# Layer 0 of a two-layer decoder trunk: twenty conv taps and seven weight low parts move to GpSimd, and the diagonal tap products leave TensorE

## The chip, the cores and the metric

The kernel runs on one core of one Trainium2 chip. A core has five engines that run side by side, each in its own order: TensorE (PE, matrix products, with weight loads PEld beside them), VectorE (DVE), ScalarE (ACT), GpSimd (POOL) and SyncE (SP, which here issues the DMAs). The metric is the device time of one execution in microseconds (us), lower being better. Times of runs are medians; the profile is of one execution.

## What is computed

Two layers over 512 tokens of 1024 channels, all in float32. The part that matters here is the mixer of layer 0:

```python
proj = h @ w_in
a, g = proj[..., :CONV_CH], proj[..., CONV_CH:c0]
u = a * jax.nn.sigmoid(g)
u = causal_dwconv(u, conv_w, conv_b)
u = jax.nn.silu(layernorm(u, conv_ln_g, conv_ln_b))
...
q = (rmsnorm(cq, q_norm_g) @ w_uq).reshape(B, S, MLA_HEADS, QK_NOPE + QK_ROPE)
...
o = mla_attention(qn, qr, kn, kr, v)
return jnp.concatenate([u, o], axis=-1) @ w_out
```

The causal depthwise convolution has 31 taps on 512 channels: each output channel is a sum of 31 shifted copies of its own input channel, each times one number. Beside it stand eight heads of causal attention, and both go through one output projection. After the mixer comes a gated MLP with a 3-tap conv; layer 1 is a pooling mixer and another MLP.

## The kernel before

Channels lie on the 128 partitions, the 512 tokens along the free dimension. Every large product is made of three: each float32 operand is split into a high part (rounded, made by ScalarE) and a low part (the rest, made by VectorE), and `mm3` (L107) issues high by high, high by low and low by high into one PSUM bank. `split` (L96) makes such a pair.

**Weights** come in chunks of up to 128x1024 in the order of `stream` (L130). `fetch` issues a chunk's DMA on SyncE, `prepare` splits it, `weights()` hands it out and keeps one chunk prepared ahead. The raw chunk, its high and its low part have three buffers each. Chunk 18 is the first of w_uq, 19 and 20 are w_ukv, 21 to 23 the other three of w_uq (called uq1, uq2, uq3 below; 768 columns; each serves the queries of two heads), 24 to 31 w_out (1024 columns).

**The convolution** has four tiles of 128 channels. `glu` (L429) makes the input u of a tile (its last step, L439, is on VectorE) and calls `conv` (L375), which puts closures on lists; `pump` takes some from the lists and so decides where in the program a tap stands. Tiles 0, 1 and 2 begin with tap 30 and the bias on ScalarE (L383, into a PSUM bank with the tag conv) and add taps 0 to 29 on VectorE (L400, one instruction a tap). `close` copies the sum to `side`. Tile 3 does taps 0 to 15 on TensorE: GpSimd makes a diagonal matrix with the tap's 128 weights (L392), and TensorE multiplies u by it in full float32 into the bank aux (L393); VectorE adds taps 16 to 30, and `close` adds the bias. Tiles 0 and 1 get their u early, tile 2 at about 85 us, tile 3 at about 97 us.

**The attention** goes head by head: `scores(h)`, for even heads the keys of the next pair (`keys_of`), `transposes(h-1)`, `queries(h+2)`, `values(h-2)`. Inside `scores`, `pump(BLK, i % 2)` takes two entries of the VectorE list after each of four blocks, and one entry of the TensorE list after every second. `queries(h)` multiplies the w_uq chunk with three tiles of the query latent.

**After the heads** the four conv tiles are transposed on TensorE (L623), normalized over the channels on VectorE (L625 to L637), transposed back (L648) and multiplied with the second half of w_out.

A scheduler puts each engine's instructions into one fixed order when the program is built; at run time an engine waits at an instruction until its inputs are there, and everything behind it on that engine waits too.

Of the kernel before, what the change touches and what calls it, by code (L numbers as in the profile page):

```python
# [8 lines left out]
F32 = mybir.dt.float32  # L9
F32R = mybir.dt.float32r  # L10
I32 = mybir.dt.int32
AF = mybir.ActivationFunctionType
ALU = mybir.AluOpType
AX = mybir.AxisListType

P = 128
S = 512
# [5 lines left out]
CW = 31  # L23
# [9 lines left out]
C_NE, C_CB, C_LG, C_LB, C_QG, C_KG, C_NO, C_PS, C_NF, C_FN = 0, 8, 12, 16, 20, 23, 25, 33, 41, 57  # L33
# [3 lines left out]
N_COL = C_FB + 2 * NF  # L37

WARM = 40
PE_TAPS = 16  # L40
W_PAD, T_PAD, R_PAD = 48, 16, 120
GLU, LAT, BLK, END = 3, 4, 2, 0

# [2 lines left out]
def kernel(  # L46
# [20 lines left out]
    act, dve, pool, pe = nc.scalar, nc.vector, nc.gpsimd, nc.tensor  # L67
# [11 lines left out]
    def uid(s):  # L79
        count[0] += 1  # L80
        return f"{s}{count[0]}"

    def bank():
        return p_ps.tile([P, S], F32, tag="ps", name=uid("ps"))

    def aux(tag="aux"):
        return p_ps.tile([P, S], F32, tag=tag, bufs=1, name=uid(tag))

    def temp():
        return p_t.tile([P, 2 + S], F32, tag="t", name=uid("t"))[:, :S]  # L90

    def small(n=4, dt=F32):
        return p_s.tile([P, 8], dt, tag=f"s{dt}", name=uid("s"))[:, :n]


    def split(dst, src):  # L96
        i = act.copy(dst[0], src)  # L97
        dve.tensor_tensor(dst[1], src, dst[0].bitcast(F32), op=ALU.subtract)  # L98
        return i

    def split_scaled(dst, src, scale):
# [40 lines left out]
    raws, ready = [], []  # L142
# [3 lines left out]
    def fetch():  # L146
        src, n = stream[len(raws)]
        raw = p_w.tile([P, 1024], F32, tag="raw", name=uid("raw"))[:, :n]
        nc.sync.dma_start(raw, src)
        raws.append(raw)  # L150

    def prepare():
        i = len(ready)
        if i == len(raws):
            fetch()
        n = stream[i][1]
        hi = p_w.tile([P, 1024], F32R, tag="hi", name=uid("hi"))[:, :n]
        lo = p_w.tile([P, 1024], F32R, tag="lo", name=uid("lo"))[:, :n]
        copied = split((hi, lo), raws[i])
        raws[i] = None  # L160
        ready.append((hi, lo))
        return copied

    def weights(ahead=1):
        given[0] += 1
        while len(ready) < min(given[0] + ahead, len(stream)):
            prepare()
        w = ready[given[0] - 1]
        ready[given[0] - 1] = None
        return w  # L170
# [18 lines left out]
    def c(i):  # L189
        return col[:, i : i + 1]  # L190

    sq = p_c.tile([P, 3, P], F32, name="sq")
    ident, ones, fold_kr = sq[:, 0, :], sq[:, 1, :], sq[:, 2, :]
# [80 lines left out]
    p_m = tc.alloc_tile_pool(name="mixer", bufs=1, side="left", reuse_waits="tile")  # L274
# [8 lines left out]
    for k in range(KD):  # L283
        xk = p_x.tile([P, S], F32, tag="x", name=uid("x"))
        nc.sync.dma_start(xk, xT[k * P : (k + 1) * P, :])
        x.append(xk)
        fetch()
        if k < 3:
            opened = prepare()
        split_scaled(pair(xg[k]), xk, c(C_NE + k))  # L290
# [63 lines left out]
    for k in range(KD):  # L354
        w = weights(2)
# [8 lines left out]
    def project():  # L364
        w = weights()
        ps = bank()
        for k in range(KD):
            mm3(ps, part(w, k), pair(xg[k]), k == 0, k == KD - 1)
        return ps

    u, ys, work, pe_work = [], [], [], []

    def conv(m):  # L375
        cw = C_CW + CW * m
        side = p_m.tile([P, S], F32, tag="side", bufs=4, name=uid("side"))
        ys.append(side)
        st = {}

        def open_acc():
            st["acc"] = aux("conv")
            act.activation(  # L383
                st["acc"], u[m][:, CW - 1 : CW - 1 + S], AF.Identity,
                bias=c(C_CB + m), scale=c(cw + CW - 1),
            )

        def pe_tap(j):
            if j == 0:
                st["acc"] = aux()  # L390
            d = p_m.tile([P, P], F32, tag="tapped", bufs=4, name=uid("tap"))
            pool.tensor_scalar(d, ident, c(cw + j), None, op0=ALU.mult)  # L392
            pe.matmul(st["acc"], d, u[m][:, j : j + S], start=j == 0, stop=j == PE_TAPS - 1)  # L393

        def tap(j):
            while m == 3 and pe_work:
                pe_work.pop(0)()
            if not st:
                open_acc()
            i = dve.scalar_tensor_tensor(  # L400
                st["acc"], u[m][:, j : j + S], c(cw + j), st["acc"],
                op0=ALU.mult, op1=ALU.add,
            )
            if held:
                tc.add_manual_dep(
                    i.ins, held.pop().ins.name,
                    mybir.DependencyInfo(
                        mybir.DependencyClass.NoSync, mybir.DependencyReason.DATA
                    ),
                    reason="background",  # L410
                )

        def close():
            bias = c(C_CB + m) if m == 3 else 0.0
            act.activation(side, st["acc"], AF.Identity, bias=bias, scale=1.0)

        n_pe = PE_TAPS if m == 3 else 0
        pe_work.extend((lambda j=j: pe_tap(j)) for j in range(n_pe))
        work.extend((lambda j=j: tap(j)) for j in range(n_pe, CW if m == 3 else CW - 1))
        work.append(close)  # L420

    def pump(nd, np_=0):
        for _ in range(min(np_, len(pe_work))):
            pe_work.pop(0)()
        for _ in range(min(nd, len(work))):
            work.pop(0)()


    def glu(ps_a, ps_g):  # L429
        t = temp()  # L430
        dve.tensor_tensor(t, ps_g, rows0, op=ALU.mult)
        s = temp()
        act.activation(s, t, AF.Sigmoid)
        if len(u) == 3:
            act.activation(spare, s[:, 0:1], AF.Exp)
        dve.tensor_tensor(s, s, rows0, op=ALU.mult)
        ut = p_m.tile([P, 640], F32, tag="u", bufs=4, name=uid("u"))[:, : CW - 1 + S]
        pool.memset(ut[:, : CW - 1], 0.0)
        dve.tensor_tensor(ut[:, CW - 1 :], ps_a, s, op=ALU.mult)  # L439
        u.append(ut)  # L440
        conv(len(u) - 1)
# [6 lines left out]
    def latent(n, gain, width):  # L448
        parts, stat = [], Squares(width, dve)
        for m in range(n):  # L450
            ps = project()
            parts.append(s4())
            split_scaled(pair(parts[m]), ps, c(gain + m))
            stat.add(ps)
            pump(LAT)
        return parts, stat
# [11 lines left out]
    for _ in range(2):  # L468
        ps_a = project()
        pump(GLU)  # L470
        ps_g = project()
        glu(ps_a, ps_g)
        pump(GLU)
    p_xg.release()
    p_a = tc.alloc_tile_pool(name="attn", bufs=1, side="right", reuse_waits="tile")
    keys = [p_m.tile([P, 2, S], F32, tag="k", bufs=2, name=f"keys{i}") for i in range(2)]
# [26 lines left out]
    def scores(h):  # L503
        q, key = qs.pop(h), keys[h // 2 % 2][:, h % 2, :]
        pb = p_a.tile([P, 1280], F32, tag="prob", bufs=3, name=uid("prob"))
        mx, nb, ls = small(), small(), small()
        blocks, at = [], 0
        for i in range(4):
            w = (i + 1) * P
            ps = bank()  # L510
            pe.matmul(ps[:, :w], q[:, i * P : (i + 1) * P], key[:, :w], start=True, stop=True)  # L511
            p = pb[:, at : at + w]
            at += w
            dve.tensor_tensor_reduce(
                out=p, in0=ps[:, :w], in1=causal[:, S - w :], scale=1.0,
                scalar=-3.0e38, op0=ALU.add, op1=ALU.max, accum_out=mx[:, i : i + 1],
            )
            blocks.append(p)
            if i % 2:
                two = slice(i - 1, i + 1)  # L520
                dve.scalar_tensor_tensor(
                    nb[:, two], mx[:, two], -1.0, q_scale[:, two], op0=ALU.mult, op1=ALU.mult
                )
                for n in (i - 1, i):
                    act.activation(
                        blocks[n], blocks[n], AF.Exp, bias=nb[:, n : n + 1],
                        scale=q_scale[:, n : n + 1], accum_out=ls[:, n : n + 1],
                    )
            pump(BLK, i % 2)
        dve.reciprocal(ls, ls)  # L530
        for i in range(4):
            act.activation(blocks[i], blocks[i], AF.Copy, scale=ls[:, i : i + 1])
        probs[h] = blocks
        sums[h] = ls[:, 3:4]
# [85 lines left out]
    for i in range(4):  # L620
# [3 lines left out]
        st = p_s.tile([P, 6], F32, tag="bn", bufs=2, name=uid("bn"))  # L624
# [11 lines left out]
    for i in range(4):  # L636
        dve.tensor_scalar(  # L637
            yts[i], yts[i], mv[:, i, 0:1], r_ln[:, i : i + 1],
            op0=ALU.subtract, op1=ALU.mult,
# [3 lines left out]
    for m in range(4):  # L643
# [5 lines left out]
        t = temp()  # L649
# [183 lines left out]
    for h in range(2):  # L833
        w = weights()
        for i in range(4):
# [11 lines left out]
            if (h, i) >= (0, 2):  # L847
                while zps:
                    i, ps = zps.pop(0)
# [151 lines left out]
```

## Time and profile before

| | |
|---|---|
| median of 3 runs | 991.12 us (990.99 to 994.11) |
| the profiled execution's own time | 992.3 us |
| its span, first to last instruction | 990.5 us |
| mean granted TensorE clock | 0.993 |
| DVE instructions, busy | 915, 591.3 us |
| POOL instructions, busy | 107, 70.7 us |

The times of single instructions below are from the profiled execution, whose own time is 1.2 us above the median. A row of a timeline gives the start in the span, the duration (of all instructions merged in the row), the engine, the line, the operation, what it writes and reads, and in brackets the idle time before it and who ended it. Durations of instructions that follow each other can overlap; the distance between two starts is then what one costs. A row of the chain gives the start, the time that the chain spent there, and the line. A row of windows gives busy time of PE, PEld, DVE, ACT and POOL in a stretch of time, each with the number of instructions, then the granted clock, the DMA share and GB/s.

### The profile page before, as it was taken

Reading aid. Unit: us, or ns where it says so; the run is one execution under the profiler, and the core shown is the slowest. Engines: PE = TensorE matmul, PEld = TensorE weight load, DVE = VectorE, ACT = ScalarE, POOL = GpSimd, SP = SyncE. Lnnn points to the kernel's source line nnn. Section 1 sums busy time; section 2 is a strip of 40 time slices with the busy share of each in tenths; the row PEclk is TensorE's granted clock in tenths of the full one; section 3 lists DMA queues with packets and bytes.
Section 4 is the critical chain, followed back from the end, with each engine's and each line's share of the span. In section 5 each row is a group of like instructions: output and inputs, shape, how many; then the busy total and the mean of one; then the engine's idle time right before and its main releaser. Section 6 shows DMA issues by size and latency. Waiting matters only on the chain.

```text
span 990.5 us, 11545 instructions
## 1 busy us (share of the span) xinstructions
PE 973.5 (98%) x4476; PEld 799.1 (81%) x4476; DVE 591.3 (60%) x915; ACT 400.6 (40%) x581; POOL 70.7 (7%) x107
## 2 busy tenths in 40 slices
PE   8999999999999999999999999999999999999996
PEld 7788676777888888888888889888888888888885
DVE  6899989847675656555332338585656565522323
ACT  6534677544343333334222236253333333332321
POOL 6000100003000000000001102200000000000111
PEclk9999999999999999999999999999999999999998
DMA  6422101113233232322323241323232323323212
GB/s 216 157 81 90 48 18 65 36 49 109 84 107 107 85 107 93 98 94 98 100 92 107 86 158 44 107 86 106 85 107 86 106 87 105 100 92 106 86 43 85
DMA packets 29478, 91.99 MB, mean 93 GB/s; under 512 B 4080, under 2 KB 6384, under 8 KB 29424
## 3 DMA queue, kind: packets, MB, share of 16 engines
q1 hardware_dynamic: 28880, 90.74, 28.1%
q8 instruction: 35, 0.57, 0.3%
q10 hardware_dynamic: 544, 0.52, 0.2%
q14 instruction: 19, 0.16, 0.0%
HBM read 89.02 MB, written 2.23 MB: 92 GB/s over the span
## 4 chain that ended last, share of the span: by engine, by line
PE 93%; DVE 4%; DMA 1%; issue 1%; SPq 0%; ACT 0%; DVEq 0%
PE ps L108 28%; PE ps L109 28%; PE ps L110 28%; PE ps L558 2%; PE ps L511 2%; DVE lo L98 1%; PE aux L393 1%; PE ps L546 1%; PE aux L261 1%; PE aux L239 1%; DMA x<-in_xT_dram 0%; DVE xgl L103 0%; DMA col<-in_cols_dram 0%; PE ps L870 0%; PE ps L869 0%
## 5 line engine op out<-in xcount | busy, mean ns | idle before, releaser
L108 PE MATMUL ps<-xgh,hi 128*128 128x512 f32 x816 | 319.3, 391 | 2.0 <-ACT hi L97 1.8
L97 ACT CAST hi<-raw 128x1024 fp32r<-128x1024 f32 (+2 forms) x166 | 170.0, 1026 | 373.7 <-PE ps L109 351.5
L110 PE MATMUL ps<-xgh,lo 128*128 128x512 f32 x816 | 318.0, 390 | 0.8 <-DVE lo L98 0.8
L109 PE MATMUL ps<-xgl,hi 128*128 128x512 f32 x816 | 318.4, 390 | 0.0
L98 DVE TENSOR_TENSOR lo<-raw,hi 128x1024 fp32r<-128x1024 f32 (+2 forms) x166 | 201.6, 1216 | 153.8 <-ACT hi L97 153.3
L108 PEld LDWEIGHTS ps<-xgh,hi 128*128 128x128 f32 x816 | 153.8, 188 | 34.5 <-ACT hi L97 2.6
L110 PEld LDWEIGHTS ps<-xgh,lo 128*128 128x128 f32 x816 | 153.5, 188 | 33.4 <-DVE lo L98 2.0
L109 PEld LDWEIGHTS ps<-xgl,hi 128*128 128x128 f32 x816 | 153.7, 188 | 31.8
L108 PE MATMUL ps<-gh,hi 128*128 128x512 f32 (+1 forms) x374 | 141.1, 377 | 0.0
L109 PE MATMUL ps<-gl,hi 128*128 128x512 f32 (+1 forms) x374 | 140.9, 377 | 0.0
L110 PE MATMUL ps<-gh,lo 128*128 128x512 f32 (+1 forms) x374 | 140.8, 376 | 0.0
L108 PEld LDWEIGHTS ps<-gh,hi 128*128 128x128 f32 x374 | 70.4, 188 | 13.0
L110 PEld LDWEIGHTS ps<-gh,lo 128*128 128x128 f32 x374 | 70.4, 188 | 13.0
L109 PEld LDWEIGHTS ps<-gl,hi 128*128 128x128 f32 x374 | 70.4, 188 | 12.7
L698 DVE TENSOR_TENSOR t<-ps,rows 128x512 f32<-128x512 f32 x44 | 30.4, 691 | 76.9 <-PE ps L110 76.9
L226 POOL TENSOR_TENSOR sqr<-sqr,sqr 128x512 f32<-128x512 f32 x33 | 50.4, 1529 | 314.4 <-ACT sqr L224 284.5
L710 DVE TENSOR_TENSOR t<-ps,rows 128x512 f32<-128x512 f32 x44 | 30.4, 690 | 67.3 <-PE ps L110 67.0
L400 DVE SCALAR_TENSOR_TENSOR conv<-u,col,conv 128x512 f32<-128x512 f32 x90 | 67.5, 750 | 1.7 <-ACT conv L383 0.7
L705 DVE SCALAR_TENSOR_TENSOR t<-t,col,t 128x512 f32<-128x512 f32 x88 | 65.7, 748 | 1.4
L708 ACT ACTIVATE t<-t 128x512 f32<-128x512 f32 x44 | 27.8, 631 | 74.4 <-DVE t L705 74.4
L103 DVE SCALAR_TENSOR_TENSOR xgl<-x,col,xgh 128x512 fp32r<-128x512 f32 x32 | 32.7, 1037 | 12.4 <-ACT xgh L102 12.3
L108 PE MATMUL ps<-s,hi 128*128 128x512 f32 x96 | 39.7, 427 | 0.0
(182 smaller groups left out, 817.1 us busy)
## 6 DMA issues: line engine op xcount, KB each, us to landing
raw<-in_w_up_dram SPq DMA_DIRECT2D x88, 512.0 KB, 3.3
raw<-in_w_down_dram SPq DMA_DIRECT2D x44, 512.0 KB, 3.3
raw<-in_w_in_dram SPq DMA_DIRECT2D x10, 512.0 KB, 3.4
raw<-in_w_out_dram SPq DMA_DIRECT2D x8, 512.0 KB, 3.3
x<-in_xT_dram SPq DMA_DIRECT2D x8, 256.0 KB, 4.4
raw<-in_w_in_dram SPq DMA_DIRECT2D x8, 256.0 KB, 3.4
raw<-in_w_uq_dram SPq DMA_DIRECT2D x4, 384.0 KB, 3.0
raw<-in_w_ukv_dram SPq DMA_DIRECT2D x2, 512.0 KB, 3.8
```

The source lines that it names most:

```text
L97: i = act.copy(dst[0], src)
L98: dve.tensor_tensor(dst[1], src, dst[0].bitcast(F32), op=ALU.subtract)
L103: dve.scalar_tensor_tensor(dst[1], src, scale, dst[0].bitcast(F32), op0=ALU.mult, op1=ALU.subtract)
L108: pe.matmul(ps, a[0], b[0], start=start, stop=False)
L109: pe.matmul(ps, a[0], b[1], start=False, stop=False)
L110: pe.matmul(ps, a[1], b[0], start=False, stop=stop)
L226: self.engine.tensor_tensor(self.parts[0], self.parts[0], t, op=ALU.add)
L400: i = dve.scalar_tensor_tensor(st["acc"], u[m][:, j : j + S], c(cw + j), st["acc"], op0=ALU.mult, op1=ALU.add,)
L698: dve.tensor_tensor(ut[:, 2 : 2 + S], pu, rows, op=ALU.mult)
L705: dve.scalar_tensor_tensor(a, ut[:, j : j + S], c(fw + j * NF + f), a, op0=ALU.mult, op1=ALU.add)
L708: act.activation(a, a, AF.Silu)
L710: dve.tensor_tensor(b, pv, rows, op=ALU.mult)
```

## The change

`PE_TAPS` goes, and with it the diagonal matrices and their products. Tile 3 is now opened on ScalarE like the other tiles. Of tiles 2 and 3, taps 0 to 9 are made by GpSimd: the first multiplies u by the tap's column, spread along the tokens, straight into `side`; the others multiply into one of two buffers and then add to `side`. VectorE makes taps 10 to 29, and `close` adds its PSUM sum to `side` there. The low parts of chunks 21 to 27 (uq1 to uq3 and four chunks of w_out) are made by GpSimd. GpSimd taps are pumped two after each gate of the second pair of tiles, then one after each score block.

```diff
-PE_TAPS = 16
+POOL_TAPS = (0, 0, 10, 10)
+POOL_LOW = range(21, 28)
...
-    def split(dst, src):
+    def split(dst, src, engine=None):
         i = act.copy(dst[0], src)
-        dve.tensor_tensor(dst[1], src, dst[0].bitcast(F32), op=ALU.subtract)
+        (engine or dve).tensor_tensor(dst[1], src, dst[0].bitcast(F32), op=ALU.subtract)
...
-        copied = split((hi, lo), raws[i])
+        copied = split((hi, lo), raws[i], pool if i in POOL_LOW else dve)
...
-        def pe_tap(j):
-            if j == 0:
-                st["acc"] = aux()
-            d = p_m.tile([P, P], F32, tag="tapped", bufs=4, name=uid("tap"))
-            pool.tensor_scalar(d, ident, c(cw + j), None, op0=ALU.mult)
-            pe.matmul(st["acc"], d, u[m][:, j : j + S], start=j == 0, stop=j == PE_TAPS - 1)
+        def pool_tap(j):
+            t = side
+            if j:
+                t = p_m.tile([P, S], F32, tag="tapped", bufs=2, name=uid("tapped"))
+            w = c(cw + j).to_broadcast([P, S])
+            pool.tensor_tensor(t, u[m][:, j : j + S], w, op=ALU.mult)
+            if j:
+                pool.tensor_tensor(side, side, t, op=ALU.add)
...
         def close():
-            bias = c(C_CB + m) if m == 3 else 0.0
-            act.activation(side, st["acc"], AF.Identity, bias=bias, scale=1.0)
-
-        n_pe = PE_TAPS if m == 3 else 0
-        pe_work.extend((lambda j=j: pe_tap(j)) for j in range(n_pe))
-        work.extend((lambda j=j: tap(j)) for j in range(n_pe, CW if m == 3 else CW - 1))
+            if n_pool:
+                dve.tensor_tensor(side, st["acc"], side, op=ALU.add)
+            else:
+                act.copy(side, st["acc"])
+
+        n_pool = POOL_TAPS[m]
+        pool_work.extend((lambda j=j: pool_tap(j)) for j in range(n_pool))
+        work.extend((lambda j=j: tap(j)) for j in range(n_pool, CW - 1))
...
-        pump(GLU)
+        pump(GLU, 2)
...
-            pump(BLK, i % 2)
+            pump(BLK, 1)
```

Lines after the first edit are one, later three, higher than before: L98 becomes L99, L400 becomes L401, L511 becomes L514.

In the order of GpSimd, the changed program has these rows from the last taps of tile 2 to the first of tile 3. `u_807` is tile 2's input and `u_889` tile 3's; `side_810` and `side_892` are their sums; `lo_979` is the low part of uq1.

```order
L394 TENSOR_TENSOR tapped_1099<-u_807,col 128x512
L396 TENSOR_TENSOR side_810<-side_810,tapped_1055 128x512
L396 TENSOR_TENSOR side_810<-side_810,tapped_1099 128x512
L394 TENSOR_TENSOR tapped_1110<-u_807,col 128x512
L396 TENSOR_TENSOR side_810<-side_810,tapped_1110 128x512
L99 TENSOR_TENSOR lo_979<-raw_976,hi_978 128x768
L394 TENSOR_TENSOR side_892<-u_889,col 128x512
L394 TENSOR_TENSOR tapped_1127<-u_889,col 128x512
```

Nineteen rows of tile 2 (ten multiplies, nine adds) stand ahead of `lo_979`; before, the low part of uq1 was VectorE's, right behind the last gate's u. The same engine ends tile 3 so, with uq2's low part (`lo_1077`), uq3's (`lo_1242`) and the first of w_out (`lo_1414`) behind all nineteen rows of tile 3:

```order
L394 TENSOR_TENSOR tapped_1302<-u_889,col 128x512
L396 TENSOR_TENSOR side_892<-side_892,tapped_1302 128x512
L99 TENSOR_TENSOR lo_1077<-raw_1074,hi_1076 128x768
L99 TENSOR_TENSOR lo_1242<-raw_1239,hi_1241 128x768
L99 TENSOR_TENSOR lo_1414<-raw_1411,hi_1413 128x1024
```

Before, the low part of uq2 (then `lo_1062`) stood on VectorE among the score blocks of head 0 (`prob_1008`):

```order
L514 ISA prob_1008,s_1009<-ps_1017,causal 128x256
L514 ISA s_1009 128x1
L98 TENSOR_TENSOR lo_1062<-raw_1059,hi_1061 128x768
L521 SCALAR_TENSOR_TENSOR s_1010<-s_1009,misc 128x2
L514 ISA prob_1008,s_1009<-ps_1029,causal 128x384
```

It has moved from the blocks of head 0 on one engine to the end of tile 3's taps on another.

On TensorE, the program before has this around scores(2), the keys (`ps_1188`), the transposes of head 1 and queries(4), which read uq2:

```order
L393 MATMUL aux_1023<-u_885,tap_1162 128x512
L511 MATMUL ps_1167<-keys_899,q_1075 128x384
L511 MATMUL ps_1172<-keys_899,q_1075 128x512
L393 MATMUL aux_1023<-u_885,tap_1178 128x512
L108 MATMUL ps_1188<-s_626,hi_903 128x512
```

and the changed one this from the last key product (`ps_1213`) over the transposes (L549) to the first product with `lo_1077`:

```order
L111 MATMUL ps_1213<-s_666,lo_914 128x512
L549 MATMUL ps_1223<-sq,prob_1092 128x128 x4
L549 MATMUL ps_1229<-sq,prob_1092 128x128 x4
L549 MATMUL ps_1235<-sq,prob_1092 128x128 x2
L109 MATMUL ps_1245<-s_502,hi_1076 128x512
L110 MATMUL ps_1245<-s_502,hi_1076 128x512
L111 MATMUL ps_1245<-s_502,lo_1077 128x512
```

The two tap products have gone from between the score blocks of each head; the other TensorE rows around the heads, queries(2) and queries(4) among them, keep their places.

More of the change, by code (lines that the diff above doesn't have):

```diff
@@ L369, in project @@
         return ps
-    u, ys, work, pe_work = [], [], [], []
+    u, ys, work, pool_work = [], [], [], []
     def conv(m):
@@ L386, in open_acc @@
             )
-        def pe_tap(j):
-            if j == 0:
-                st["acc"] = aux()
-            d = p_m.tile([P, P], F32, tag="tapped", bufs=4, name=uid("tap"))
-            pool.tensor_scalar(d, ident, c(cw + j), None, op0=ALU.mult)
-            pe.matmul(st["acc"], d, u[m][:, j : j + S], start=j == 0, stop=j == PE_TAPS - 1)
+        def pool_tap(j):
[6 more added lines that the diff above has]
+                pool.tensor_tensor(side, side, t, op=ALU.add)
         def tap(j):
-            while m == 3 and pe_work:
-                pe_work.pop(0)()
             if not st:
@@ L413, in close @@
         def close():
-            bias = c(C_CB + m) if m == 3 else 0.0
-            act.activation(side, st["acc"], AF.Identity, bias=bias, scale=1.0)
-        n_pe = PE_TAPS if m == 3 else 0
-        pe_work.extend((lambda j=j: pe_tap(j)) for j in range(n_pe))
-        work.extend((lambda j=j: tap(j)) for j in range(n_pe, CW if m == 3 else CW - 1))
+            if n_pool:
[5 more added lines that the diff above has]
+        work.extend((lambda j=j: tap(j)) for j in range(n_pool, CW - 1))
         work.append(close)
     def pump(nd, np_=0):
-        for _ in range(min(np_, len(pe_work))):
-            pe_work.pop(0)()
+        for _ in range(min(np_, len(pool_work))):
+            pool_work.pop(0)()
         for _ in range(min(nd, len(work))):
```

## The prediction

> **What bounds the kernel now.** I read the engine totals and the engine shares of the chain that ended last first, then busy time by stretches of the attention stage, then that stage's timelines engine by engine.
>
> ```profile
> PE 973.5 (98%) x4476; PEld 799.1 (81%) x4476; DVE 591.3 (60%) x915; ACT 400.6 (40%) x581; POOL 70.7 (7%) x107
> PE 93%; DVE 4%; DMA 1%; issue 1%; SPq 0%; ACT 0%; DVEq 0%
> 84.00:108.00 24.00, 24.00 (x106) 18.88 (x105) 22.71 (x38) 13.24 (x21) 1.29 (x1) 1.00 0.22 72
> 108.00:128.00 20.00, 20.00 (x87) 14.05 (x86) 19.45 (x48) 14.75 (x39) 3.02 (x5) 1.00 0.17 52
> 128.00:158.00 30.00, 30.00 (x127) 20.32 (x126) 27.15 (x64) 23.23 (x54) 3.62 (x6) 1.00 0.07 22
> ```
>
> TensorE sets the time: 98% busy, 93% of the chain. The averages hide that in the attention stage, where the change sits, VectorE is nearly as full (in the last three rows TensorE, its weight loads, VectorE, ScalarE, GpSimd: VectorE busy 22.71 of 24, 19.45 of 20, 27.15 of 30 us), while GpSimd is almost empty. So the stage has two near-equal limits, and the change fills the empty engine.
>
> **What goes from TensorE.**
>
> ```profile
> 105.60 0.86 PE aux L393 x2
> 161.89 0.86 PE aux L393 x2
> L393 PE MATMUL aux<-u,tap x32: 592/592/594, 105.4 to 168.4; 128*128 128x512 f32 x32
> ```
>
> The diagonal taps are 32 matmul instructions, two for each of 16 taps, and one tap holds the chain for 0.86 us: 16 x 0.86 = **13.8 us** of TensorE, at two taps a head. Six come before queries(4), ten after.
>
> **What goes to GpSimd.** 20 multiplies and 18 adds of 128x512, in two runs of 19 (tile 2, then tile 3), and seven low parts. The program before has no multiply by a column spread over 512 elements there, but it has two-input adds.
>
> ```profile
> L226 POOL TENSOR_TENSOR sqr<-sqr,sqr x33: 1279/1616/2149, 10.7 to 963.9; 128x512 f32<-128x512 f32 x33
> 13.76 3.12 POOL L226 TENSOR_TENSOR sqr<-sqr,sqr 128x512 f32<-128x512 f32 x2
> 15.12 3.45 POOL L226 TENSOR_TENSOR sqr<-sqr,sqr 128x512 f32<-128x512 f32 x2
> L769 POOL TENSOR_TENSOR gl<-x,t x4: 726/736/747, 975.5 to 985.4; 128x256 f32<-128x256 f32 x4
> L343 POOL MEMSET ctab<- 64x512 f32 x1 | 0.5, 519 | 0.0
> ```
>
> An undisturbed add takes 1.28 to 1.29 us, and two that follow each other start 15.12 - 13.76 = 1.36 us apart. I take 1.36 us for all 38. A multiply is bounded below by the 0.52 us of a memset, which reads nothing; above, by the 1.70 us of the next rows. It is nearest to the add, since it too names two tensors. From 736 ns for 256 columns to 1.29 us for 512, a column costs 2.16 ns, so a low part of 768 columns is 1.29 + 256 x 0.00216 = 1.84 us, one of 1024 2.4 us.
>
> ```profile
> 613.44 1.63 POOL L226 TENSOR_TENSOR sqr<-sqr,sqr 128x512 f32<-128x512 f32 x1
> 615.15 3.33 POOL L226 TENSOR_TENSOR sqr<-sqr,sqr 128x512 f32<-128x512 f32 x2
> 613.83 0.74 DVE L665 SCALAR_TENSOR_TENSOR x<-ps,col,x 128x512 f32<-128x512 f32 x1
> 614.50 1.13 DVE L103 SCALAR_TENSOR_TENSOR xgl<-x,col,xgh 128x512 fp32r<-128x512 f32 x1
> L98 DVE TENSOR_TENSOR lo<-raw,hi 128x1024 fp32r<-128x1024 f32 x154 | 190.8, 1240 | 152.9 <-ACT hi L97 152.5 <-issue 0.3
> L98 DVE TENSOR_TENSOR lo<-raw,hi 128x768 fp32r<-128x768 f32 x4 | 3.8, 952 | 0.4 <-ACT hi L97 0.4
> L400 DVE SCALAR_TENSOR_TENSOR conv<-u,col,conv 128x512 f32<-128x512 f32 x90 | 67.5, 750 | 1.7 <-ACT conv L383 0.7
> ```
>
> Here VectorE and GpSimd collide. L103 reads two tensors in SBUF and takes 1.13 us beside a GpSimd add; L665, with one input in PSUM, keeps its 0.74. The adds move from 1.36 to 615.15 - 613.44 = 1.71 us apart: 0.35 for each collision. The Trainium skill ("SBUF — State Buffer", Who interferes with whom) has this as a rule: a VectorE instruction with two SBUF inputs contends with a GpSimd instruction that reads SBUF, and the second fully blocks. By the rule the conv taps would collide with nothing, and the trace agrees in that with L665; it does not in how long the block lasts, since L103's 0.74 became 1.13 and not 0.74 plus a whole add of 1.29. By full blocking each collision would cost GpSimd a whole VectorE instruction, and the sum below would grow by about 1 us.
>
> The conv taps read u in SBUF and keep their sum in PSUM, as L665 has one input in each, so I let them run free. Only two low parts that stay on VectorE (1024 wide) and one product of the gate meet tile 2's run. A 1024-wide low part is 0.5 us longer than L103: 2 x 0.8 + 0.35 = 1.9 us.
>
> **When the low parts are ready, and when TensorE wants them.** GpSimd runs in order. uq1's low part stands behind the whole tile 2 run, uq2's and uq3's behind the whole tile 3 run. The run starts when u of tile 2 is written (L439).
>
> ```profile
> 84.77 0.68 DVE L439 TENSOR_TENSOR u<-ps,t 128x512 f32<-128x512 f32 x1
> 110.49 0.39 PE L110 MATMUL ps<-s,lo 128*128 128x512 f32 x1
> 125.94 0.40 PE L110 MATMUL ps<-s,lo 128*128 128x512 f32 x1
> ```
>
> The second row is the first product with uq1's low part (queries(2)), the third that with uq2's (queries(4)).
> - uq1: 85.5 + 19 x 1.36 + 1.9 + 1.84 = **115.1**. TensorE, two taps lighter, wants it at 110.5 - 1.7 = 108.8: it waits 6.3 us.
> - uq2: 115.1 + 19 x 1.36 + 1.84 = **142.8**. TensorE wants it at 115.1 + (125.9 - 110.5) - 4 x 0.86 = 127.1: it waits 15.7 us.
>
> Behind the waiting matmul stand, in TensorE's order, scores(1) and scores(3), the transposes and all later queries; VectorE stops at the query product that reads the same bank, and ScalarE behind both. GpSimd's remaining low parts (uq3, four of w_out) follow at 1.84 to 2.4 us each and are wanted later: no cost.
>
> ```profile
> raw<-in_w_out_dram SPq DMA_DIRECT2D x8, 512.0 KB, 3.3
> 175.93 0.39 PE L110 MATMUL ps<-s,lo 128*128 128x512 f32 x1
> ```
>
> SyncE's queue is touched too: with three buffers for raw weights, the load of w_out's first chunks can start only when uq1's, uq2's and uq3's low parts have been made, so at 115, 143 and 145 instead of 98, 107 and 122. They land 3.3 us later, and the first is wanted at 175.9, now later still: no cost.
>
> From there on only ten taps are saved: 142.8 - 125.9 - 10 x 0.86 = **+8.3 us**.
>
> **What else moves.**
>
> ```profile
> 16.27 0.50 PE L108 MATMUL ps<-xgh,hi 128*128 128x512 f32 x1 [1.82 <-ACT hi L97]
> 18.64 0.63 PE L108 MATMUL ps<-xgh,hi 128*128 128x512 f32 x1
> 19.07 0.63 PE L109 MATMUL ps<-xgl,hi 128*128 128x512 f32 x1
> 20.70 0.40 PE L108 MATMUL ps<-xgh,hi 128*128 128x512 f32 x1
> 20.94 0.39 PE L109 MATMUL ps<-xgl,hi 128*128 128x512 f32 x1
> ```
>
> After a wait of 1.82 us TensorE ran matmuls 0.43 us apart until 19.9, then 0.23: some nine at 0.20 extra, **+1.8 us**. A wait of 16 us should end the same way, and only the second one's slow start counts (the first lies inside the second wait). Ends: 0 and 3.6.
>
> ```profile
> 157.07 0.65 DVE L500 TENSOR_TENSOR q<-ps,ctab 128x512 f32<-128x512 f32 x1
> 178.66 8.66 DVE L400 SCALAR_TENSOR_TENSOR aux<-u,col,aux 128x512 f32<-128x512 f32 x11
> 188.92 0.60 PE L623 MATMUL aux<-sq,side 128*128 128x128 f32 x4
> 192.24 1.03 DVE lo L98
> 198.46 0.30 PE L648 MATMUL aux<-sq,t 128*128 128x128 f32 x1 [1.16 <-DVE t L637]
> ```
>
> From the last query (157.1) to the transposes of the conv result (188.9) VectorE had 30 taps and one low part. It now has 29 taps, no low part (1.1 less), two closing adds (0.6 each) and a wait for ScalarE to open tile 3's sum once tile 2's bank is free (some 1 us): as long as before, while TensorE lost four taps (3.4 us). So most of those four pay nothing: **+2.5 us**, between 0 and 3.4. Against it, one of two low parts on the chain into the layer norm (192.24) leaves VectorE, where TensorE then waits 1.16: **-1.0 us**. The other savings on VectorE (five taps, six low parts, some 10 us) are hidden under TensorE's wait.
>
> **Sum.** 8.3 + 1.8 + 2.5 - 1.0 = +11.6 us. The profiled execution took 992.3 us (span 990.5 and 1.8 around it), 1.2 above the median of 991.1; so 1003.9 beside it, and **1003 us** as a median. Its own ends: all 38 at 1.29 us and no collision (-4.6) and no slow clock (-1.8) give 996; 38 steps of 1.50 us, half way to 1.70 (+5.3), and a slow clock of 3.6 (+1.8) give 1010.
>
> **The rivals.**
> 1. *Faster: the multiply is cheap.* If GpSimd reads the spread column once, its 20 multiplies cost less than an add. Each 0.1 us less brings both runs in 2 us sooner in all. The sum reaches zero where a multiply takes 1.36 - 11.6 / 20 = 0.78 us; at the memset's 0.52 it is 11.6 - 16.8 = -5.2, so 986 us. For it: no row shows this form. Against: the operand is still a tensor of 512 elements. The Trainium skill ("GPSIMD Engine Reference", 3.1 Elementwise) gives 769 ns as the best case of a loop over 512 elements and puts `tensor_tensor` at 2.6 cycles an element, since its two inputs share one read port. By the first figure the whole would end, as an estimate, at 991; the adds of 1.29 us agree with the second.
> 2. *Slower still: conv taps collide too.* If every GpSimd instruction shares its time with a tap, all 38 run 1.70 us apart: 142.8 + 38 x 0.34 - 1.9 = 153.8, so 11 us more, 1014. L665's 0.74 speaks against it.
> 3. *No wait at all.* TensorE keeps its 13.8 us, less the 2.5 at the end and 1.0 more gained: 979. It needs both low parts some 16 us sooner, so 38 instructions at 0.9 us. No row of this size is that short.
>
> **How the numbers follow.** Forecast (TensorE waits behind both runs, 996 to 1010) 0.75; rival 1 0.12, half of it faster and half within 0.3%; rival 2 0.10; rival 3 0.03. A measurement of this kernel can tell 0.3%, 3 us, from no change. From 992 to 1013 lie the forecast, half of rival 2 and the upper end of rival 1, about 0.8. Faster 0.06 + 0.03 = 0.09, same 0.06, slower 0.75 + 0.10 = 0.85.
>
> **What would show it.** The first low-part matmul of queries(2) and of queries(4) waits on GpSimd's low part, some 6 and 16 us, the second much the longer; GpSimd is busy without a gap from 85 to about 145; its 128x512 instructions start 1.3 to 1.4 us apart; matmuls 0.43 us apart follow the second wait; L401's taps stay at 0.75 us. It is wrong if multiplies last under 0.8 us, if the low parts land before 121 us, or if TensorE waits elsewhere.

## The result, and the profile after

| kernel | median | runs | ratio to before, 95% interval |
|---|---|---|---|
| before | 991.69 us (990.99 to 994.11) | 5 | |
| changed | 1000.47 us (1000.18 to 1000.52) | 5 | 1.0082 [1.0070, 1.0093] |

The change costs 8.8 us. The span of the profiled execution grew by 8.0, from 990.5 to 998.5 us, so that the trace has nearly all of it. The same stretches of the attention stage as before (TensorE, its weight loads, VectorE, ScalarE, GpSimd, then the granted clock), of the changed kernel, and under them TensorE's waits from 84 to 220 us (for what, in total, how often, the longest):

```profile
84.00:108.00 24.00, 23.51 (x106) 18.84 (x106) 23.53 (x34) 12.67 (x18) 21.10 (x17) 1.00 0.17 50
108.00:128.00 20.00, 16.67 (x71) 12.00 (x69) 18.45 (x46) 14.21 (x38) 19.69 (x18) 0.91 0.08 27
128.00:158.00 30.00, 21.80 (x88) 15.75 (x89) 16.75 (x41) 16.32 (x39) 12.13 (x9) 0.83 0.17 53
...
PE ps L111 <- POOL lo L99: 11.5, 2, 9.6
PE aux L651 <- DVE t L640: 1.8, 1, 1.8
PE ps L561 <- ACT pt L551: 1.1, 1, 1.1
PE ps L549 <- ACT prob L535: 0.9, 1, 0.9
```

TensorE had no idle time here; now it is idle for 3.3 and 8.2 us in the second and third stretch, and almost all of it is two waits for a low part from GpSimd. GpSimd itself is full until the second of them ends. Its groups, then its timeline at the two places, then TensorE's:

```profile
L396 POOL TENSOR_TENSOR side<-side,tapped 128x512 f32<-128x512 f32 x18 | 25.6, 1421 | 0.8
L394 POOL TENSOR_TENSOR tapped<-u,col 128x512 f32<-128x512 f32 x18 | 18.4, 1040 | 0.0
...
86.59 1.04 POOL L394 TENSOR_TENSOR side<-u,col 128x512 f32<-128x512 f32 x1 [63.91 <-DVE u L442]
87.59 2.04 POOL L394 TENSOR_TENSOR tapped<-u,col 128x512 f32<-128x512 f32 x2
...
110.86 1.80 POOL L99 TENSOR_TENSOR lo<-raw,hi 128x768 fp32r<-128x768 f32 x1
112.62 1.04 POOL L394 TENSOR_TENSOR side<-u,col 128x512 f32<-128x512 f32 x1
...
115.62 2.63 POOL L396 TENSOR_TENSOR side<-side,tapped 128x512 f32<-128x512 f32 x2
...
134.34 3.58 POOL L99 TENSOR_TENSOR lo<-raw,hi 128x768 fp32r<-128x768 f32 x2
...
112.72 0.50 PE L111 MATMUL ps<-s,lo 128*128 128x512 f32 x1 [1.98 <-POOL lo L99]
...
113.32 0.63 PE L110 MATMUL ps<-s,hi 128*128 128x512 f32 x1
113.75 0.63 PE L111 MATMUL ps<-s,lo 128*128 128x512 f32 x1
...
136.20 0.79 PE L111 MATMUL ps<-s,lo 128*128 128x512 f32 x1 [9.55 <-POOL lo L99]
136.79 0.63 PE L109 MATMUL ps<-s,hi 128*128 128x512 f32 x1
137.22 0.63 PE L110 MATMUL ps<-s,hi 128*128 128x512 f32 x1
...
139.35 2.91 PE L561 MATMUL ps<-pt,v 128*128 128x512 f32 x8
...
147.44 2.32 PE L561 MATMUL ps<-pt,v 128*128 128x512 f32 x8
```

Each low part stands behind a run of 19 tap instructions. The tile 2 run lasts from 86.59 to 110.86, the tile 3 run from 112.62 to 134.34; the low parts follow at once, and the two matmuls start as they end (each takes 1.8 us). queries(4) starts its low product at 136.20, 10.3 us later than before. The matmuls behind it stand 0.43 us apart, and eight products with the values last 2.91 us, where the next eight last 2.32.

### The profile page after: what moved, and what is told of

The parts are those of the page before. It is cut to its first block, busy times and chain, and to the rows that moved or that the text cites. A ratio compares the mean times of both kernels' runs of the same rounds, so it can differ in the third digit from the quotient of the medians.

```text
span 998.5 us, 11503 instructions
## 1 busy us (share of the span) xinstructions
PE 965.3 (97%) x4444; PEld 794.3 (80%) x4444; DVE 587.8 (59%) x905; ACT 400.5 (40%) x580; POOL 119.3 (12%) x136
## 4 chain that ended last, share of the span: by engine, by line
PE 81%; DVE 3%; issue 1%; ACT 1%; DVEq 0%
PE ps L109 26%; PE ps L111 25%; PE ps L110 25%; PE ps L561 1%; PE ps L514 1%; DVE lo L99 1%; DVE conv L401 0%; DVE xgl L104 0%; PE ps L549 0%; PE aux L262 0%; PE aux L240 0%; PE ps L873 0%; PE ps L872 0%; DVE x L666 0%; ACT prob L528 0%
## 5 line engine op out<-in xcount | busy, mean ns | idle before, releaser
L98 ACT CAST hi<-raw 128x1024 fp32r<-128x1024 f32 (+2 forms) x166 | 170.0, 1027 | 375.5 <-PE ps L110 335.0
L99 DVE TENSOR_TENSOR lo<-raw,hi 128x1024 fp32r<-128x1024 f32 (+2 forms) x159 | 195.5, 1231 | 153.6 <-ACT hi L98 153.3
L401 DVE SCALAR_TENSOR_TENSOR conv<-u,col,conv 128x512 f32<-128x512 f32 x100 | 75.0, 750 | 2.3 <-ACT conv L384 0.9
L700 POOL MEMSET t<- 128x2 f32 x44 | 4.3, 100 | 422.9 <-DVE t L714 350.3
L111 PE MATMUL ps<-s,lo 128*128 128x512 f32 x96 | 39.3, 409 | 11.5 <-POOL lo L99 11.5
```

Source lines behind the costliest of these rows:

```text
L99: (engine or dve).tensor_tensor(dst[1], src, dst[0].bitcast(F32), op=ALU.subtract)
L111: pe.matmul(ps, a[1], b[0], start=False, stop=stop)
L401: i = dve.scalar_tensor_tensor(st["acc"], u[m][:, j : j + S], c(cw + j), st["acc"], op0=ALU.mult, op1=ALU.add,)
```

## The experiments

Two theories had to be told apart first. **Order**: the loss is the place of the low parts in GpSimd's queue, so it goes when they no longer stand behind taps. **Sharing**: GpSimd's taps slow VectorE, whatever the queue is. A third, that a low part on GpSimd is itself too slow, has one kernel of its own.

**All low parts back on VectorE, taps left on GpSimd.**

```diff
-POOL_LOW = range(21, 28)
+POOL_LOW = ()
```

> The changed kernel with all seven low parts back on VectorE; the twenty GpSimd taps stay. Theory (order): TensorE lost its time to uq1's and uq2's low parts standing behind 19 and 38 tap instructions on GpSimd, so without them there the waits of 2.0 and 9.6 us and the slow clock behind them (1.8) go: 1000.5 - 13.4 = 987, plus up to 4 us because VectorE, which is nearly full, gets 8 us of low parts back: 985 to 991. Rival (sharing): what costs is that GpSimd and VectorE hold each other up for 60 us, whatever GpSimd does; then it stays within 3 us of 1000. Rival (slow low parts): a low part at 1.8 to 2.4 us on GpSimd is itself too slow; gives 985 to 991 here too.

**Only uq1 to uq3 back.**

```diff
-POOL_LOW = range(21, 28)
+POOL_LOW = range(24, 28)
```

> The changed kernel with only uq1's, uq2's and uq3's low parts back on VectorE; w_out's four stay on GpSimd. Theory (order): both waits of TensorE on GpSimd go, VectorE gets 2.6 us back in the heads: 984 to 989, at or below the run with all seven back. Rival (sharing): within 3 us of 1000. In the layer norm the VectorE low part beside GpSimd's low part of the fourth w_out chunk should still take 2.3 us instead of 1.2.

Measured: 992.28 us, ratio 1.0002 [0.9992, 1.0013], and 991.15 us, 0.9990 [0.9979, 1.0001]. Both waits for GpSimd are gone and so is the loss, which speaks for order. But both are above what was expected: TensorE has no diagonal taps here, and nothing was gained. Its waits in the first of the two are for VectorE and for ScalarE behind it (the low part of the layer norm took 2.32 us in the second, as expected):

```profile
PE aux L651 <- DVE t L640: 4.5, 1, 4.5
PE ps L549 <- ACT prob L535: 2.8, 5, 1.0
```

**The low parts alone, on the kernel before; its diagonal taps stay.**

```diff
+POOL_LOW = range(21, 28)
...
-        dve.tensor_tensor(dst[1], src, dst[0].bitcast(F32), op=ALU.subtract)
+        (engine or dve).tensor_tensor(dst[1], src, dst[0].bitcast(F32), op=ALU.subtract)
...
-        copied = split((hi, lo), raws[i])
+        copied = split((hi, lo), raws[i], pool if i in POOL_LOW else dve)
```

> The kernel before with only the seven low parts moved to GpSimd; TensorE keeps its 16 diagonal taps and GpSimd has no taps of its own. Theory (order): a low part on a GpSimd that has nothing else to do is in time, TensorE waits for none, and TensorE is the limit: 989 to 993. Rival (slow low parts): TensorE waits 1 us or more at each of queries(2), queries(4) and queries(6) and its clock drops: 995 or more.

Measured: 990.27 us, 0.9980 [0.9970, 0.9991], as expected, and TensorE waits for none of these low parts. With no taps ahead of it in the queue, a low part of 768 columns that takes 1.82 us on GpSimd (0.95 on VectorE) is in time. The third theory falls.

**Both on GpSimd, low parts first.** Each GpSimd multiply is ordered behind the last low part that the program gave GpSimd before it; the work is the same.

```diff
+    ahead = []
...
+        low = (engine or dve).tensor_tensor(dst[1], src, dst[0].bitcast(F32), op=ALU.subtract)
+        if engine is pool:
+            ahead[:] = [low]
...
-            pool.tensor_tensor(t, u[m][:, j : j + S], w, op=ALU.mult)
+            i = pool.tensor_tensor(t, u[m][:, j : j + S], w, op=ALU.mult)
+            if ahead:
+                tc.add_manual_dep(
+                    i.ins, ahead[0].ins.name,
...
```

> The changed kernel with the same work on every engine, but each GpSimd multiply is held behind the last low part that the program made before it, so that uq1's low part stands behind 7 tap instructions instead of 19, uq2's behind 15 instead of 38, uq3's behind 30 instead of 38. Theory (order): TensorE waits for no low part; 1000.5 - 13.4 = 987, between 982 and 989, at or below the run with the three back on VectorE. Rival (sharing): the same work collides as before, within 3 us of 1000. Rival (slow low parts): between 993 and 1000.

Measured: 989.73 us, 0.9979 [0.9968, 0.9991]. Order alone is worth some 10 us (1.0082 to 0.9979): the same instructions on the same engines, and the loss is gone. But the time is 0.7 us over the upper end of what was expected: of TensorE's 13.8 us only 2 are gained. This run's windows, TensorE's largest wait, and the group of a small VectorE product (L536 here, L524 in the changed kernel: minus the row maximum times the scale, two a head, each the bias of two exponentials):

```profile
108.00:128.00 20.00, 18.86 (x87) 13.54 (x86) 19.79 (x45) 15.16 (x40) 19.76 (x18) 1.00 0.08 27
128.00:158.00 30.00, 27.60 (x122) 18.91 (x120) 29.12 (x65) 24.96 (x57) 17.14 (x12) 1.00 0.21 71
...
PE ps L561 <- ACT prob L547: 3.8, 6, 1.6
...
L536 DVE SCALAR_TENSOR_TENSOR s<-s,misc 128x2 f32<-128x2 f32 x16 | 10.1, 629 | 0.1
...
107.49 0.96 DVE L536 SCALAR_TENSOR_TENSOR s<-s,misc 128x2 f32<-128x2 f32 x1
123.62 1.29 DVE L536 SCALAR_TENSOR_TENSOR s<-s,misc 128x2 f32<-128x2 f32 x1
149.85 0.15 DVE L536 SCALAR_TENSOR_TENSOR s<-s,misc 128x2 f32<-128x2 f32 x1
```

VectorE is 99% and 97% busy although it has less to do. The small product takes 0.15 us when GpSimd rests (last row) and up to the length of a GpSimd instruction when it does not: 10.1 us for sixteen, where they need 16 x 0.155 = 2.5. In the two kernels with low parts back on VectorE the sixteen had taken 6.4 and 8.5 us, too. New theory: VectorE is held up by GpSimd in this product, and so gives back what it saved. Rival: VectorE simply has too much work. The next two kernels keep "low parts first" and take the collision away in two ways.

**The product on ScalarE** (a column copy with a scale; the factor is made once).

```diff
-                dve.scalar_tensor_tensor(
-                    nb[:, two], mx[:, two], -1.0, q_scale[:, two], op0=ALU.mult, op1=ALU.mult
-                )
+                for n in (i - 1, i):
+                    act.activation(
+                        nb[:, n : n + 1], mx[:, n : n + 1], AF.Copy,
+                        scale=misc[:, 20 + n : 21 + n],
+                    )
```

> Low parts first as in the run before (989.7 us), and the small 128x2 product ahead of the exponentials (two operands in SBUF, 0.15 us alone, up to 2.26 us beside GpSimd) is made on ScalarE as two one-column copies with a scale. Theory, VectorE is held up by GpSimd in its instructions with two SBUF operands: VectorE gets back the 7.6 us by which nine of these products were longer, less what lies beside TensorE's own work; 983 to 987, and TensorE's waits on the exponentials (3.8 us) go. Rival, VectorE simply has too much work and the taps behind the last head set the end: 988.5 to 991, no gain.

**The product on VectorE, as two one-column instructions with one tensor operand.**

```diff
+                for n in (i - 1, i):
+                    dve.tensor_scalar(
+                        nb[:, n : n + 1], mx[:, n : n + 1], misc[:, 20 + n : 21 + n], None,
+                        op0=ALU.mult,
+                    )
```

> The same product stays on VectorE, as two one-column tensor_scalar instructions: one tensor operand and a per-partition scalar in place of two tensors. If it is the second tensor operand that is held up, each takes 0.1 to 0.15 us beside GpSimd as well and the time comes to 983 to 988; if any small VectorE instruction waits for GpSimd, they take 0.3 to 2 us and the time is 989 to 993, as before or worse.

Measured: 984.23 us, 0.9928 [0.9914, 0.9942], and 985.22 us, 0.9937 [0.9925, 0.9950]. Both times are as the theory had it. TensorE's waits on the exponentials did not go altogether: 1.1 us are left in the first (3.8 before) and 2.5 in the second. In the second the product lies at the same place on the same engine, in twice as many instructions, and none of the 32 is held:

```profile
L537 DVE TENSOR_SCALAR s<-s,misc x32: 183/208/214, 107.7 to 171.4; 128x1 f32<-128x1 f32 x32
```

Their shortest, median and longest are 183, 208 and 214 ns, a little over the 0.1 to 0.15 that was expected, with GpSimd busy and without. So in this product it is the second tensor operand that GpSimd holds up, not the small size. Between the two forms the instruction changed as well, but the conv taps are `scalar_tensor_tensor` like the held product, with one operand in PSUM, and were not held either (0.75 us, see below). That one tensor operand is always safe does not follow: the last kernel of this section has an exception.

**Controls**: the product on ScalarE in the kernel before, and in the changed kernel in its own order (same edit).

> A control: the kernel before, where GpSimd has nothing to do in the heads and the small 128x2 product takes 0.155 us each time (2.5 us in sixteen), with that product on ScalarE as two one-column copies. If moving it paid 5 us above because it no longer meets GpSimd, here it pays at most its own 2.5 us: 989.5 to 992.5. Rival, the move pays by itself, whatever GpSimd does (a shorter way to the exponentials): 986 to 988, as 5 us less.

> The changed kernel in its own order, with the small product on ScalarE. Its sixteen took 5.2 us beside GpSimd in place of 2.5. Order theory: TensorE's two waits for low parts (2.0 and 9.6 us) stay, since GpSimd's queue is the same, and no more than the 2.7 us come back: 997 to 1000.5. Rival, the small product held by GpSimd is what delays the heads and the wait is only where it shows: 990 to 995, as with the low parts first.

Measured: 991.89 us, 0.9996 [0.9988, 1.0005], and 1000.32 us, 1.0078 [1.0065, 1.0091]. The move pays nothing where GpSimd rests, and nothing where TensorE waits for GpSimd's queue anyway:

```profile
PE ps L111 <- POOL lo L99: 11.4, 2, 9.4
```

So the changed kernel loses its time by order alone, and the collisions are what would stop the gain once the order is mended.

**What a multiply costs GpSimd.** Two variants of the changed kernel, each with another convolution of tiles 2 and 3 than the reference's: the multiply with a full tile in place of the spread column, and the adds turned into multiplies on the same tiles.

```diff
-            pool.tensor_tensor(t, u[m][:, j : j + S], w, op=ALU.mult)
+            pool.tensor_tensor(t, u[m][:, j : j + S], u[m][:, 0:S], op=ALU.mult)
```

> The changed kernel with the second operand of GpSimd's tap multiply a full 128x512 tile of u in place of the broadcast weight column, so the convolution of the last two tiles is another one than the reference's. If the 1.04 us of the multiply (where 1.36 was forecast) comes from the broadcast operand, each takes 1.25 to 1.4 us, the low part that uq2 waits for comes 3 to 4 us later and the span is 1001 to 1004. If a multiply takes 1.04 us whatever its operand is, nothing moves: 998 to 999.

```diff
-                pool.tensor_tensor(side, side, t, op=ALU.add)
+                pool.tensor_tensor(side, side, t, op=ALU.mult)
```

> The changed kernel with GpSimd's 18 adds into side made multiplies into side, same operands and same tile written, so the convolution of the last two tiles is another one than the reference's. If the operation sets the price (a multiply 1.04 us, an add 1.29), they take 1.04 us undisturbed, the low part that uq2 waits for comes some 18 x 0.28 = 5 us sooner, and the span is 993 to 996. If reading and writing the same tile sets it, they stay at 1.29 us and nothing moves: 998 to 999.

Measured, in one execution each: spans of 998.5 and 998.6 us; by group (shortest, median and longest in ns; the first row is of the first kernel, the second of the second):

```profile
L394 POOL TENSOR_TENSOR tapped<-u x18: 1025/1044/1301, 86.5 to 131.7; 128x512 f32<-128x512 f32 x18
...
L396 POOL TENSOR_TENSOR side<-side,tapped x18: 1261/1286/2280, 88.6 to 132.1; 128x512 f32<-128x512 f32 x18
```

Neither the spread column nor the operation makes the difference: a multiply of two full operands out of the same tile takes 1.04 us, and a multiply into `side` takes as long as the add did. What does, two different tiles to read or writing one that is read, no run of 512 columns separates. The low parts point to the first: they read two tiles and write a third, and from their means of 1.81 us for 768 columns and 2.37 for 1024, 512 columns would take 1.25 us, as an estimate, which is about the add's price.

**A version that beats both.** Low parts first, the product on ScalarE, six more taps of tile 3 on GpSimd, and the last w_out low part on VectorE; then the same with that low part on GpSimd.

```diff
-POOL_TAPS = (0, 0, 10, 10)
-POOL_LOW = range(21, 28)
+POOL_TAPS = (0, 0, 10, 16)
+POOL_LOW = range(21, 27)
```

> Low parts first, the small product on ScalarE, 16 taps of tile 3 on GpSimd in place of 10 (six more in the time in which it was idle), and the last w_out low part back on VectorE. Theory that VectorE sets the stretch behind the last head: six taps by 0.75 us are 4.5 us less there, and the 2.3 us collision at the last low part goes, so 4 to 6 us below the run with the product on ScalarE: 978 to 982. Rival, GpSimd's longer run holds VectorE up in the heads by as much: 983 to 988. Below 985 it beats both kernels.

> The best version so far (978.4 us) with the last w_out low part on GpSimd again, the one edit. If VectorE's layer-norm low part beside it (2.32 us in place of 1.21) and GpSimd's 2.4 us stand on the path: 979.5 to 981.5, and TensorE waits 1.7 to 2.2 us for the normalized tile. If the six moved taps were the whole gain: 978 to 979.

Measured: **978.44 us**, 0.9873 [0.9858, 0.9887], and 980.50 us, 0.9880 [0.9865, 0.9895]. The first is 13 us below the kernel before, close to the 13.8 us that TensorE was relieved of. The two intervals overlap, so what the last low part costs is open. The second kernel's time lies in the range that was forecast, but not for the reason given: VectorE's low part was not beside GpSimd's, which had been expected, and TensorE waited 0.8 us where 1.7 to 2.2 were expected. GpSimd's low part (184.48 to 187.07) met the normalization instead, four instructions with one tensor operand and two columns. The first row is of the first kernel, the others of the second:

```profile
182.99 1.92 DVE L654 TENSOR_SCALAR t<-t,misc,s 128x512 f32<-128x512 f32 x4
...
184.48 2.59 POOL L101 TENSOR_TENSOR lo<-raw,hi 128x1024 fp32r<-128x1024 f32 x1 [24.45 <-ACT hi L100]
184.28 3.98 DVE L654 TENSOR_SCALAR t<-t,misc,s 128x512 f32<-128x512 f32 x4
```

One of the four lasts 2.61 us, the others 0.53 to 0.55, so an instruction with one tensor operand can be held too; what sets it apart from the small product is not shown.

The product on ScalarE alone and the second kernel differ by the six taps only: 984.23 and 980.50 us, and their intervals do not overlap. The taps are then most of the 5.8 us by which the first kernel lies below the product on ScalarE alone. The first kernel's windows:

```profile
108.00:128.00 20.00, 20.00 (x97) 15.09 (x96) 18.99 (x47) 19.54 (x57) 19.77 (x18) 1.00 0.07 27
128.00:158.00 30.00, 29.51 (x135) 20.75 (x133) 27.84 (x65) 29.72 (x79) 29.69 (x24) 1.00 0.13 40
```

TensorE is full again, and in the second stretch ScalarE (29.72 of 30 us) and GpSimd (29.69) are too; VectorE's 27.84 is the only slack left there.

## Why the prediction came out as it did

The forecast was 1003 us in a range of 992 to 1013; 1000.47 was measured, in the main by the mechanism that was forecast: TensorE waits for the low parts behind both runs of taps. Its steps against the trace, as the delay against the kernel before at four places:

| place | forecast, step | measured, step |
|---|---|---|
| first low product of queries(4) | +16.9 | +10.3 |
| query product of the last head | -5.2 + 1.8 = -3.4 | -2.2 |
| first statistics of the conv result | -3.4 + 2.5 = -0.9 | +0.8 |
| end of the span | -1.0 | -0.9 |
| sum | +11.6 | +8.0 |

The rows for the second and third place: the first is of the kernel before, whose last query product (157.07) stands in the prediction, the others are of the changed one:

```profile
189.56 0.70 DVE L625 BATCH_NORM_STATS2 bn<-aux 128x6 f32<-128x512 f32 x1 [0.77 <-PE aux L623]
...
165.13 0.68 DVE L503 TENSOR_TENSOR q<-ps,ctab 128x512 f32<-128x512 f32 x1
...
198.46 0.70 DVE L628 BATCH_NORM_STATS2 bn<-aux 128x6 f32<-128x512 f32 x1 [0.68 <-PE aux L626]
```

**GpSimd's step of 1.36 us: the term that was mis-sized.** An add fits (two last 2.6 us undisturbed), but a multiply starts 1.00 us after the one before (86.59, 87.59). A run is 10 x 1.00 + 9 x 1.31 = 21.8 us, not 25.8, and the undisturbed one took 21.7. The uq2 low part was ready at 136.2, not at 142.8: 3.5 us of it come from the first run, 4.1 from the second, less 1.1 because the first began later. That is rival 1 part of the way, far from its break-even of 0.78 us, and not for its reason, since the spread column saves nothing. The Trainium skill ("GPSIMD Engine Reference", 3.1 Elementwise) has 2.6 cycles an element at 1.2 GHz for `tensor_tensor`, by which 512 elements are, as an estimate, 1.11 us; the multiply's 1.04 us agrees with that better than the adds do, which the prediction had set beside it, and the best case of 769 ns was not reached in these runs.

**The waits.** Two, the second much the longer, as forecast; 2.0 and 9.6 us in place of 6.3 and 15.7, for the same cause. The run with the low parts first shows that they are the loss.

**The slow clock.** Forecast 1.8 us; seven matmuls from 136.20 to 139.35 at 0.20 extra and the eight products 0.59 longer make 2.0, with a granted clock of 0.63 from 136.2 to 142.1 us. The step would then be -5.2 + 2.0 = -3.2, and it is -2.2. About half of the difference lies with VectorE: TensorE's last queries start 7.5 us later than before (161.92, where it was 154.39), VectorE's product on them 8.1 later. The rest was not traced.

**The last stretch.** This term was mis-sized too: +2.5 was said to be lost of TensorE's 3.4 us, and it is all of it and 0.8 more. VectorE sets this stretch, as was said, and the prediction's own reading, that VectorE's part is as long as before, asks for the whole 3.4 and not for 2.5. The 0.8 is mostly in the taps. There are 29 in place of 30, as was counted, but they take as long. The first two rows are of before:

```profile
171.05 0.74 DVE L400 SCALAR_TENSOR_TENSOR aux<-u,col,aux 128x512 f32<-128x512 f32 x1
171.71 0.74 DVE L400 SCALAR_TENSOR_TENSOR conv<-u,col,conv 128x512 f32<-128x512 f32 x1
...
178.91 1.55 DVE L401 SCALAR_TENSOR_TENSOR conv<-u,col,conv 128x512 f32<-128x512 f32 x2 [0.79 <-ACT conv L384]
...
186.80 8.66 DVE L401 SCALAR_TENSOR_TENSOR conv<-u,col,conv 128x512 f32<-128x512 f32 x11
...
L416 DVE TENSOR_TENSOR side<-conv,side 128x512 f32<-128x512 f32 x2 | 1.4, 689 | 0.1
```

A tap that is followed by something else than a tap on the same sum costs some 0.66 us from start to start (171.05, 171.71); eleven in a row on one sum take 8.66, 0.79 each. Before, taps of tiles 2 and 3 took turns on two sums; now tile 3's sum opens when tile 2's is closed, so that fifteen taps in place of ten stand right behind another on their own sum. Five times 0.13 us are 0.65, nearly the tap that was saved. The other terms came close to what was counted (a wait of 0.79 us for ScalarE where 1 was said, two adds of 0.69 where 0.6 was).

Moving six taps from VectorE to GpSimd, and nothing else, brought the time down from 984.23 to 980.50 us in the experiments, which shows the bound. This error and the mis-sized multiply go opposite ways, so the total is nearer than its parts.

**The low part in the layer norm**: forecast -1.0, measured -0.9, but not by the mechanism that was forecast, so that the agreement is luck. One low part left VectorE, and the one that stayed was held up by GpSimd's last one. The first three rows are of before:

```profile
191.62 0.70 DVE L625 BATCH_NORM_STATS2 bn<-aux 128x6 f32<-128x512 f32 x1 [0.49 <-PE aux L623]
192.24 1.21 DVE L98 TENSOR_TENSOR lo<-raw,hi 128x1024 fp32r<-128x1024 f32 x1
194.04 1.21 DVE L98 TENSOR_TENSOR lo<-raw,hi 128x1024 fp32r<-128x1024 f32 x1
...
198.61 2.38 POOL L99 TENSOR_TENSOR lo<-raw,hi 128x1024 fp32r<-128x1024 f32 x1 [31.01 <-ACT hi L98]
...
199.76 2.32 DVE L99 TENSOR_TENSOR lo<-raw,hi 128x1024 fp32r<-128x1024 f32 x1
```

Two low parts of 1.21 us have become one of 2.32: nothing is saved there, and TensorE's wait for the normalized tile grew from 1.16 to 1.8 us. Of the 0.9, 0.6 are gained between the first statistics and the normalization (189.56 to 197.76 before, 198.46 to 206.06 now), most of it VectorE's wait of 0.49 us for the transposes, which is gone; where the last 0.3 come from was not traced.

**What collides.** "Only two low parts and one product of the gate" was too few. The first run lost 2.6 us to collisions (24.3 against 21.7), where 1.9 were forecast, and the small product L524 was held too, 5.2 us for sixteen in place of 2.5:

```profile
L524 DVE SCALAR_TENSOR_TENSOR s<-s,misc 128x2 f32<-128x2 f32 x16 | 5.2, 322 | 0.1
```

In the changed kernel this costs nothing that can be measured, as the control shows: TensorE's wait covers it. So the prediction's number did not suffer, but **rival 3 was mispriced** by it. Without the wait the time is 989.7 us and not 979, because what VectorE saved is then given back; 979 needs the collision out of the way and the last stretch relieved. The length of the block was misread as well: L103 in the prediction's rows ends at 615.63, 0.56 us after the add that it met (613.44 and 1.63 long), so its 1.13 us leave room for a wait until that add had ended, and do not speak against a full block.

**Rival 2** falls: the conv taps, with one operand in PSUM, kept 0.75 us beside GpSimd all along, as in the kernel before:

```profile
L401 DVE SCALAR_TENSOR_TENSOR conv<-u,col,conv 128x512 f32<-128x512 f32 x100 | 75.0, 750 | 2.3 <-ACT conv L384 0.9
```

## What to carry to other kernels

An in-order engine that is nearly idle is not free to take work: ask for each piece what will stand ahead of it in that queue and when its reader wants it, since two pieces of 1.8 us, behind runs of 24 and 22 us, made a change that takes 13.8 us from TensorE cost 8.8 us here, and putting them first won some 10. Then look at what the newly busy engine holds up on its neighbour, small instructions too: a 0.15 us product with two tensor operands took up to 1.29 us beside a tap, and the cure was to write it with one tensor operand, or to move it. Last, count the work of the new bound in the stretch that ends the stage before counting what the old bound has lost.

## What was not expected of the hardware

- A VectorE instruction of two elements a partition waited for the end of the GpSimd instruction that was running when it started. In the run with the low parts first, the product at 107.49 lasts 0.96 us, until 108.45, and the one at 123.62 lasts 1.29, until 124.91; the adds beside them end at 108.44 and 124.90:

```profile
105.80 2.64 POOL L408 TENSOR_TENSOR side<-side,tapped 128x512 f32<-128x512 f32 x2
122.24 2.66 POOL L408 TENSOR_TENSOR side<-side,tapped 128x512 f32<-128x512 f32 x2
```

  This agrees with the exclusive lock in "SBUF — State Buffer", Who interferes with whom, of the Trainium skill. The same product with one tensor operand and a column was never held (214 ns at most), but one normalization of 128x512 with one tensor operand was (2.61 us for 0.54).
- GpSimd's price for 512 float32 columns depends on which tiles it reads and writes (1.04 or 1.29 us), and in these runs neither on add or multiply nor on whether the second operand is spread.
- The slow matmuls that the prediction had read after a wait of 1.82 us came after short and long waits alike: 0.43 us apart after 2.0 us (113.32 to 113.75) as after 9.6 us (136.79 to 137.22).
